# A two-layer diffusion backbone on one core: unread products at the start, two weights loaded earlier, a short softplus chain moved

## The chip, the core and the metric

The program runs on one core of a Trainium2 chip. The core has five engines that each take their own queue of instructions in order: TensorE (PE in the profile, its weight loads PEld), VectorE (DVE), ScalarE (ACT), GpSimd (POOL) and SyncE (SP). SP issues nearly all transfers between memory and the core here. An engine waits for another one, or for a transfer, at a semaphore. The metric is the device time of one execution in microseconds; less is better. TensorE's array has two clock levels in these traces, 1.2 and 2.4 GHz.

## What is computed

The reference runs two layers over 256 context tokens and 512 latent tokens of width 1024. Cut to what matters for the start of the first layer:

```python
shift, scale, gate = _adaln(c, ada_w[layer], ada_b[layer])      # silu(c) @ w + b, three parts
shift_c, scale_c, gate_c = _adaln(c_ctx, ada_w[layer], ada_b[layer])
h_l = _rmsnorm(x, norm_g[layer]) * (1.0 + scale[:, None]) + shift[:, None]
h_c = _rmsnorm(cx, norm_g[layer]) * (1.0 + scale_c) + shift_c
z = jnp.concatenate([h_c, h_l], axis=1) @ w_in                  # first step of the even mixer
...
log_a = -LRU_C * r.astype(jnp.float32) * jax.nn.softplus(-lam.astype(jnp.float32))
```

Everything after that (latent attention, the recurrent scan, the second layer's neighbourhood attention, the output projections and the final norm) is the same before and after the change.

## The kernel before

Tokens lie along the free axis and channels on the 128 partitions, so the input is eight tiles `x0` to `x7` of 128x768, with columns 0 to 511 for the latent (LAT) and 512 to 767 for the context (CTX). A product that wants nearly float32 accuracy is made of three passes in a fast format: weights and activations are split into a high part (`h`, a rounded copy, on ScalarE) and a low part (`l`, the rest, on VectorE), and `z_t` (L141) adds high x high, high x low and low x high into one PSUM tile. Such a pass is a pair of products, one with 512 columns and one with 256. For each 128 outputs there are 8 blocks k of channels, so 24 pairs.

The start of the program, which is all that the change touches, goes as follows.

1. SP loads `x0` to `x7`, then weights. A modulation chunk is two transfers of 512 KB (`ada.._0r` and `ada.._4r`).
2. ScalarE squares the x tiles and VectorE adds them up (`acc`, L365). TensorE sums over channels (`pssum`, L296), a root and its reciprocal follow, and TensorE spreads them over the partitions (`r00b`, L322). That gives `rsb`.
3. TensorE multiplies the conditioning vectors by the modulation weights (`psada`, L215, 32 outputs wide, float32). ScalarE copies the result (`rows`, L227), TensorE turns it (`psc`, L232), VectorE makes shift and factor of it (`av`, `as`, `am`, L234 to L250). `ada_prep1`/`ada_go1` do so for one block of channels; `ada_prep`/`ada_go` for a whole chunk pair, which gives two blocks: chunks 1 and 5 give blocks 2 and 3, chunks 2 and 6 give 4 and 5, chunks 3 and 7 give 6 and 7.
4. `hb(j, c)` makes block j of the modulated input: VectorE scales x (L338), ScalarE adds the shift and rounds (`hh`, L340), VectorE makes the rest (`hl`, L341).
5. TensorE multiplies each block, as it comes, by three weights: `w0t0` (into `psx0`), `w0t1` (`psx1`) and `w0t8` (`psg8`). These 72 pairs are here called the first three projections. After them VectorE copies `psx0` out (`lx0`, L537, L539), and only then may `psx2`, which uses the same PSUM banks, begin.
6. `softplus` of the recurrence's decay is a chain of 18 operations of VectorE on 128x8 values (`sp`, L504 to L515). Its result is first read by the gates of the recurrence, after the first projections.

The code names the order in which work is asked for, and a scheduler in the framework moves instructions within each engine's queue; `behind(engine)` and `issue_after(instruction)` keep it from moving work ahead of a given instruction. What the queue of each engine holds in the end is fixed when the program is built.

Of the kernel before, what the change touches and what calls it, by code (L numbers as in the profile page):

```python
# [11 lines left out]
F32 = mybir.dt.float32  # L12
# [4 lines left out]
ALU = mybir.AluOpType  # L17
# [29 lines left out]
def build(nc, tc, A, out, dbg=None):  # L47
# [4 lines left out]
    V, S, P, G, SY = nc.vector, nc.scalar, nc.tensor, nc.gpsimd, nc.sync  # L52
    PE, ACT, DVE = mybir.EngineType.PE, mybir.EngineType.Activation, mybir.EngineType.DVE

    def f(ap):
        return ap.bitcast(F32)

    def dump(name, ap):
        if dbg is not None and name in dbg:
            SY.dma_start(dbg[name], ap)  # L60
# [3 lines left out]
    def pool(name, bufs, **kw):  # L64
        cm = tc.tile_pool(name=name, bufs=bufs, reuse_waits="tile", **kw)
        p = cm.__enter__()
        pools.append((name, cm))
        return p
# [28 lines left out]
    def small(tag, name, n=1, dt=F32):  # L97
        return sm.tile([128, n], dt, tag=tag, name=name, bufs=SM.get(tag))

    HE = (G,)  # L100
    HTN = 2
    FE = V
# [3 lines left out]
    vec = cst.tile([128, NV], F32, name="vec")  # L106
    SY.dma_start(vec, A["vecs"])
    junk = cst.tile([128, 768], BF16, name="junk")

    def col(i, n=1):  # L110
        return vec[:, i : i + n]

    def load_w(name, src, shape, new=None):
        raw = (new or t4)(name + "r", shape, F32, "r")
        SY.dma_start(raw, src)
        return raw

    def split_raw(name, raw, shape, new=None, eng=V, heng=S):
        hi = (new or t4)(name + "h", shape, F32R, "h")
        if heng is S:  # L120
            S.activation(hi, raw, AF.Copy)
        else:
            heng.tensor_copy(hi, raw)
        lo = (new or t4)(name + "l", shape, F32R, "l")
        eng.tensor_tensor(lo, raw, f(hi), ALU.subtract)
        return hi, lo

    def split_w(name, src, shape, new=None, eng=V, heng=S):
        return split_raw(name, load_w(name, src, shape, new), shape, new, eng, heng)

    def kfun(hl, n=None):
        h, l = hl
        return (lambda k: h[:, k], lambda k: l[:, k])
# [19 lines left out]
    pzz2 = pool("pzz2", 1, space=PSUM)  # L153
    pa = pool("pa", 2, space=PSUM)
    pzz3 = pool("pzz3", 1, space=PSUM)
    zpools, zcount = [pzz, pzz2], [0]

    def zz(name):
# [9 lines left out]
    def ada_load(l, ch, new=None, step=4):  # L168
        return [
            load_w(f"ada{l}_{ch}_{k}", A["ada"][l, ch, :, k : min(k + step, 8)], (min(step, 8 - k), 256), new)  # L170
            for k in range(0, 8, step)
        ]
# [25 lines left out]
    def behind(*engines):  # L198

        stack = ExitStack()  # L200
        for e in engines:
            stack.enter_context(tc.issue_after(next(i for i in reversed(nc.cur_bb.bb.instructions) if i.engine == e)))
        return stack
# [38 lines left out]
    def ada_cols(l, j, raws, pp, pin=False, n=2):  # L242

        step = ada_rows(l, j, raws, pp, pin, n)
        yield next(step)
        v = next(step)
        V.tensor_tensor(ashf[l][:, j : j + n], v[:, :, 0:2], bc2(vec, V_ADAB + 24 * l + j, n), ALU.add)
        d = amul[l][:, j : j + n]
        V.tensor_tensor(d, v[:, :, 2:4], bc2(badd, 24 * l + 8 + j, n), ALU.add)
        V.tensor_tensor(d, d, bc2(vec, V_NG + 8 * l + j, n), ALU.mult)  # L250
# [84 lines left out]
    def h_block(l, j, c, x, rsb, hh, hl, pieces):  # L335

        a, s = amul[l][:, j, c : c + 1], ashf[l][:, j, c : c + 1]
        V.scalar_tensor_tensor(x, x, a, rsb, ALU.mult, ALU.mult)  # L338
        for i, o in pieces:
            S.activation(o(hh), i(x), AF.Identity, bias=s)  # L340
            V.scalar_tensor_tensor(o(hl), i(x), s, f(o(hh)), ALU.add, ALU.subtract)  # L341
# [35 lines left out]
    wt = {}  # L377

    def prep_t(ft):
        wt[ft] = kfun(split_w(f"w0t{ft}", A["w0t"][ft], (8, 128)))  # L380

    def x_t(ft):
        ps = zz(f"psx{ft}")
        z_t(both(ps), wt.pop(ft), hh, hl, 8)
        return ps
# [3 lines left out]
    def ada_prep(ch):  # L389
        ada_w[ch] = ada_load(0, ch, t4a)  # L390
# [5 lines left out]
    def ada_prep1(j):  # L396
        ada_w["half", j] = [[load_w(f"ada0{j}{m}", A["ada0"][j, m], (8, 128), t4a)] for m in range(2)]

    def ada_go1(j):
        for _ in ada_cols(0, j, ada_w.pop(("half", j)), paa, n=1):  # L400
            pass

    def hb(j, c):
        w = (LAT, CTX)[c]
        pc_ = [(lambda ap: ap, lambda ap: ap[:, w])]
        h_block(0, j, c, x_tiles[j][:, w], rsb0[:, w], hh[j], hl[j], pc_)
# [13 lines left out]
    norm0c = norm0()  # L420
    hh = [th(f"hh{j}", F32R) for j in range(8)]
    hl = [th(f"hl{j}", F32R) for j in range(8)]
    raw0 = load_w("w0t0", A["w0t"][0], (8, 128))
    ada_prep1(1)
    ada_go1(0)
    hb(0, 0)
    norm0c()
    with behind(PE, ACT):
        wt[0] = kfun(split_raw("w0t0", raw0, (8, 128)))
        hb(0, 1)  # L430
        ada_prep(1)
        ada_go1(1)
    hb(1, 0)
    hb(1, 1)
    ada_prep(5)
    ada_prep(2)
    ada_go(1)
# [11 lines left out]
    hb(5, 0)  # L449
    hb(5, 1)  # L450
    hb(6, 0)
    prep_t(1)
    hb(6, 1)
    hb(7, 0)
    hb(7, 1)
    prep_t(8)
    psx.append(x_t(0))
    psx.append(x_t(1))
    psg8 = zz3("psg8")
# [37 lines left out]
    sp4 = cst.tile([128, 8], F32, name="sp4")  # L497
    nsp4 = cst.tile([128, 8], F32, name="nsp4")

    nl, e, z, w, q = (small("sp", f"sp{i}", 8) for i in range(5))  # L500
    V.tensor_scalar(nl, col(V_LAM, 8), -1.0, None, ALU.mult)
    V.tensor_tensor(e, nl, col(V_LAM, 8), ALU.min)
    S.activation(e, e, AF.Exp)
    V.tensor_scalar(z, e, 2.0, None, ALU.add)  # L504
    V.reciprocal(z, z)
    V.tensor_tensor(z, z, e, ALU.mult)
    V.tensor_tensor(w, z, z, ALU.mult)
    V.tensor_scalar(q, w, 1.0 / 19, None, ALU.mult)
    for d in range(17, 1, -2):
        V.scalar_tensor_tensor(q, q, 1.0 / d, w, ALU.add, ALU.mult)  # L510
    V.scalar_tensor_tensor(q, q, 1.0, z, ALU.add, ALU.mult)
    V.tensor_scalar(nl, nl, 0.0, None, ALU.max)
    V.scalar_tensor_tensor(sp4, q, 2.0, nl, ALU.mult, ALU.add)
    V.tensor_scalar(nsp4, sp4, -4.0, None, ALU.mult)
    V.tensor_scalar(sp4, sp4, 4.0, None, ALU.mult)  # L515
    dump("sp4", sp4)

    SEG = ((0, NC), (NC, NT))
# [1323 lines left out]
```

## Time and profile before

| | us |
|---|---|
| median of 3 runs | 779.3 (778.96 to 779.54) |
| the profiled execution's own time | 780.51 |
| its span, first to last instruction | 778.7 |
| TensorE busy in the span | 742.4 (95%) |
| VectorE, ScalarE, GpSimd busy | 507.5, 415.6, 163.7 |

The profiled execution took 1.8 us more than its span, which lies before the first and behind the last instruction. Times inside the trace count from the start of the span. A row of the timeline stands for several equal instructions in sequence; its length runs from the start of the first to the end of the last, and on TensorE the last one's end lies behind the start of the next row, since products are pipelined. The price of a row there is the distance from its start to the next row's start.

### The profile page before, as it was taken

The numbers are of one execution on the slowest core, as the hardware profiler recorded it, in microseconds if no ns is written. First come the engines' busy times: TensorE is split into PE (matmuls) and PEld (weight loads), VectorE is DVE, ScalarE is ACT, GpSimd is POOL, SyncE is SP. The second block draws the span as 40 slices with busy tenths as digits, with TensorE's granted clock in tenths as the row PEclk, the third lists the DMA queues.
The fourth block names the chain that finished last, engine by engine and source line by source line (L and its number), as shares of the span: only waits on it lengthen the run. The fifth ranks groups of instructions, "written<-read, shape, count | busy, mean of one in ns | idle before, by whom it ended". The sixth has DMA issues, their size and how long they took to land.

```text
span 778.7 us, 13220 instructions
## 1 busy us (share of the span) xinstructions
PE 742.4 (95%) x4966; PEld 652.8 (84%) x4966; DVE 507.5 (65%) x1051; ACT 415.6 (53%) x811; POOL 163.7 (21%) x191
## 2 busy tenths in 40 slices
PE   2999999999999999999999999999999999999995
PEld 2678898787788877888998899888888799889995
DVE  5748499887478777753396567546653766568544
ACT  5424867964467777542245355535542645456633
POOL 0000002003153477404210022002200211021414
PEclk9999999999999999999999999999999999999998
DMA  8913403411455553257021550236124541336203
GB/s 332 407 49 109 134 28 122 162 42 28 118 157 141 177 169 126 89 172 261 28 82 46 144 163 16 91 113 190 38 99 140 174 120 55 109 102 170 82 1 109
DMA packets 33598, 95.29 MB, mean 122 GB/s; under 512 B 4608, under 2 KB 6784, under 8 KB 33536
## 3 DMA queue, kind: packets, MB, share of 16 engines
q1 hardware_dynamic: 32960, 93.93, 37.5%
q8 instruction: 39, 0.64, 0.3%
q10 hardware_dynamic: 576, 0.52, 0.2%
q14 instruction: 23, 0.19, 0.1%
HBM read 73.99 MB, written 4.19 MB: 100 GB/s over the span
## 4 chain that ended last, share of the span: by engine, by line
PE 75%; DVE 12%; ACT 5%; issue 4%; DMA 3%; POOL 1%; SPq 0%; POOLq 0%; ACTq 0%; DVEq 0%
PE psg L141 11%; PE psv L1270 8%; PE psq L141 7%; PE w0oy L1175 7%; PE pskl L141 6%; PE psx L141 4%; PE w1oy L1175 4%; PE pt L1387 3%; PE pskc L141 3%; PE psada L215 2%; PE s L1346 2%; PE s L808 2%; PE s L1347 2%; PE po L1370 2%; PE po L1371 2%
## 5 line engine op out<-in xcount | busy, mean ns | idle before, releaser
L764 POOL TENSOR_SCALAR p<-p,rc 128x512 f32<-128x512 f32 (+1 forms) x96 | 77.7, 812 | 325.8 <-DVE rc L763 309.7
L1354 ACT ACTIVATE p<-s,nm 128x512 f32<-128x512 f32 x64 | 43.8, 686 | 37.0 <-DVE nm L1352 20.6
L1390 DVE TENSOR_TENSOR ptl<-pt,pth 128x512 fp32r<-128x512 f32 x64 | 43.6, 687 | 26.7 <-ACT pth L1389 26.7
L1389 ACT ACTIVATE pth<-pt 128x512 fp32r<-128x512 f32 x64 | 37.3, 595 | 34.7 <-PE pt L1387 25.5
L1352 DVE CUSTOM_DVE_ANT_1 s<-s,bias 128x512 f32<-128x512 f32 x48 | 33.2, 696 | 16.3 <-PE s L1347 14.3
L1387 PE MATMUL pt<-ident,p 128*128 128x128 f32 x256 | 40.0, 272 | 0.0
L615 POOL TENSOR_TENSOR mix<-mix,la 128x256 f32<-128x256 f32 x4 | 3.6, 905 | 172.8 <-DVE la L609 124.8
L844 DVE TENSOR_TENSOR pt<-pt,pt 128x512 fp32r<-128x512 f32 x48 | 31.9, 681 | 11.5 <-ACT pt L843 11.4
L843 ACT ACTIVATE pt<-pt 128x512 fp32r<-128x512 f32 x48 | 27.4, 595 | 16.1 <-PE pt L881 16.0
L763 DVE RECIPROCAL rc<-rs 128x1 f32<-128x1 f32 x96 | 15.2, 158 | 31.6 <-ACT p L1354 22.2
L1346 PE MATMUL s<-k,q 128*128 128x256 f32 x128 | 34.3, 292 | 0.4 <-DMA q<-qx 0.2
L812 ACT ACTIVATE p<-s,nm 128x768 f32<-128x768 f32 x32 | 28.8, 901 | 10.7 <-DVE nm L810 10.4
L1387 PEld LDWEIGHTS pt<-ident,p 128*128 128x128 f32 x256 | 31.1, 140 | 4.0 <-issue 0.4
L810 DVE TENSOR_REDUCE nm<-s 128x1 f32<-128x768 f32 x32 | 30.4, 951 | 4.6 <-PE s L808 4.1
L1347 PE MATMUL s<-k,q 128*128 128x256 f32 x128 | 33.3, 284 | 0.0
L1370 PE MATMUL po<-pth,v 128*128 128x256 f32 (+1 forms) x96 | 31.6, 335 | 0.0
L1371 PE MATMUL po<-ptl,v 128*128 128x256 f32 (+1 forms) x96 | 29.6, 324 | 0.0
L881 PE MATMUL pt<-ident,p 128*128 128x128 f32 x192 | 28.7, 273 | 0.0
L862 PE MATMUL po<-pt,v 128*128 128x256 f32 x96 | 26.1, 296 | 1.7 <-DVE pt L844 1.6
L861 PE MATMUL po<-pt,v 128*128 128x256 f32 x96 | 26.6, 294 | 0.4 <-DVE rcc L763 0.4
L1346 PEld LDWEIGHTS s<-k,q 128*128 128x128 f32 x128 | 24.3, 190 | 3.0 <-issue 1.4
L1200 ACT ACTIVATE sq<-xr 128x512 f32<-128x512 f32 (+1 forms) x16 | 8.2, 522 | 33.1 <-DVE xr L1181 27.1
(966 smaller groups left out, 2636.8 us busy)
## 6 DMA issues: line engine op xcount, KB each, us to landing
ada_0r<-ada SPq DMA_DIRECT2D x22, 512.0 KB, 5.0
ada_4r<-ada SPq DMA_DIRECT2D x22, 512.0 KB, 5.4
q<-qx SPq DMA_DIRECT2D x32, 256.0 KB, 5.0
bias<-bias SPq DMA_DIRECT2D x16, 256.0 KB, 2.7
x<-xin SPq DMA_DIRECT2D x8, 384.0 KB, 6.3
xr<-xin SPq DMA_DIRECT2D x8, 384.0 KB, 7.0
x1d<-xr SPq DMA_DIRECT2D x8, 256.0 KB, 5.2
x<-x1d SPq DMA_DIRECT2D x8, 256.0 KB, 4.2
```

The costliest lines, as they stand in the source:

```text
L141: P.matmul(ps, a(k), b[k][:, c], start=(k == 0 and i == 0), stop=(k == nk - 1 and i == 2),)
L764: G.tensor_scalar(p, p, rc, 0.5, ALU.mult, ALU.mult)
L1175: P.matmul(ps, a, b[k][:, c], start=(n == m == 0 and ps is dst[0][0] and not second), stop=(n == 7 and m == 2), skip_group_check=True,)
L1270: P.matmul(ps, tok(a[k], t), b[:, k % 4], start=(k == 0 and i == 0), stop=(k == 7 and i == 2))
L1346: P.matmul(s[:, :256], lhs, kap, start=(i == 0), stop=False, skip_group_check=True)
L1347: P.matmul(s[:, 256:], lhs, k2[:, CTX], start=False, stop=(i == 1), skip_group_check=True)
L1354: S.activation(p, s, AF.Exp, bias=nm, scale=-1.0, accum_out=rsum)
L1370: P.matmul(dst, vv, h, start=first, stop=False, skip_group_check=True)
L1371: P.matmul(dst, vv, l, start=False, stop=last, skip_group_check=True)
L1387: P.transpose(ps[:, 128 * j : 128 * j + 128], p1[hd, b][:, 128 * c : 128 * c + 128], ident)
L1389: S.activation(h, ps, AF.Copy)
L1390: V.tensor_tensor(l, ps, f(h), ALU.subtract)
```

## The change

Three edits.

- 51 products of 128x512 in bf16, of a tile `junk` that GpSimd fills with ones, stand first in TensorE's queue. They write a PSUM tile that nothing reads.
- `w0t1` and `w0t8` are loaded (`load0t`) right behind the single-block modulation weights, ahead of the whole chunks, and their split (`split0t`) stands behind block 1 of h. Before, the code asked for them behind block 6, and the scheduler moved them up to where the queues below show them.
- All but the first two VectorE operations of softplus stand behind the last `hl` of block 7 (`h_mark`). Before, the scheduler had put them at the front, between the sums of squares.

```diff
+    WARM = 51
...
     junk = cst.tile([128, 768], BF16, name="junk")
+    G.memset(junk[:, :512], 1.0)
...
+    idle = pa.tile([128, 512], F32, tag="a", name="idle")
+    for _ in range(WARM):
+        P.matmul(idle, junk[:, :128], junk[:, :512], start=True, stop=True)
...
-    raw0 = load_w("w0t0", A["w0t"][0], (8, 128))
+    raw = {}
+
+    def load0t(ft):
+        raw[ft] = load_w(f"w0t{ft}", A["w0t"][ft], (8, 128))
+
+    def split0t(ft):
+        wt[ft] = kfun(split_raw(f"w0t{ft}", raw[ft], (8, 128)))
+
+    load0t(0)
     ada_prep1(1)
+    load0t(1)
+    load0t(8)
     ada_go1(0)
     hb(0, 0)
     norm0c()
     with behind(PE, ACT):
-        wt[0] = kfun(split_raw("w0t0", raw0, (8, 128)))
+        split0t(0)
         hb(0, 1)
         ada_prep(1)
         ada_go1(1)
     hb(1, 0)
     hb(1, 1)
+    with behind(DVE):
+        split0t(8)
+    split0t(1)
     ada_prep(5)
...
     hb(6, 0)
-    prep_t(1)
     hb(6, 1)
     hb(7, 0)
     hb(7, 1)
-    prep_t(8)
+    h_mark = next(i for i in reversed(nc.cur_bb.bb.instructions) if i.engine == DVE)
...
-    V.tensor_scalar(z, e, 2.0, None, ALU.add)
...
+    with tc.issue_after(h_mark):
+        V.tensor_scalar(z, e, 2.0, None, ALU.add)
...
```

The scheduler answers to these edits with another order of TensorE's queue as well. The place that matters most is where the second-last step of the modulation, `psc0_6` (it turns the result of chunks 3 and 7, from which blocks 6 and 7 of h are made), stands among the products. In the kernel before it stands inside the products of block 4:

```order
L141 MATMUL psg8_539<-hh4_189,w0t8h_437 128x512
L141 MATMUL psx0_441<-hh4_189,w0t0h_249 128x256
L141 MATMUL psx1_490<-hh4_189,w0t1h_422 128x256
L141 MATMUL psg8_539<-hh4_189,w0t8h_437 128x256
L232 MATMUL psc0_6_403<-ident_67,rows0_6_401 128x128 x2
L141 MATMUL psx0_441<-hl4_197,w0t0h_249 128x512
L141 MATMUL psx1_490<-hl4_197,w0t1h_422 128x512
```

In the changed kernel (line numbers there are a few higher):

```order
L221 MATMUL psada0_6_449<-ada0_7_4r_414,c34_162 32x256 x4
L143 MATMUL psx1_543<-hh5_243,w0t1l_355 128x512
L143 MATMUL psx1_543<-hh5_243,w0t1l_355 128x256
L143 MATMUL psg8_592<-hl5_251,w0t8h_349 128x256
L143 MATMUL psg8_592<-hh5_243,w0t8l_351 128x512
L143 MATMUL psg8_592<-hh5_243,w0t8l_351 128x256
L238 MATMUL psc0_6_468<-ident_67,rows0_6_466 128x128 x2
L143 MATMUL psx0_494<-hh6_244,w0t0h_306 128x512
L143 MATMUL psx1_543<-hh6_244,w0t1h_353 128x512
```

So `psc0_6` now stands behind all products of blocks 0 to 5, directly ahead of the first product that reads block 6. The four halves of chunks 3 and 7 (`psada0_6`), which stood in a row before, now stand one by one among the products of blocks 3 to 5. Those of chunks 1 and 5 stand one by one as well, where three of them stood in a row, and three of chunks 2 and 6, which stood one by one, now stand in a row behind `psc0_2`.

On VectorE, at the end of the modulated input, the kernel before goes straight from block 7 to the copy of `psx0`:

```order
L341 SCALAR_TENSOR_TENSOR hl7_200<-x7_102,as0_116,hh7_192 128x256
L537 COPY lx0_645<-psx0_441 128x256
L539 COPY lx0_645<-psx0_441 128x8x48
L539 COPY lx0_645<-psx0_441 128x8x2x8
L125 TENSOR_TENSOR w0t2l_672<-w0t2r_668,w0t2h_670 128x1024
```

The changed kernel has the chain of softplus between them:

```order
L347 SCALAR_TENSOR_TENSOR hl7_253<-x7_155,as0_169,hh7_245 128x256
L523 TENSOR_SCALAR sp2_673<-sp1_672 128x8
L531 TENSOR_SCALAR sp0_671<-sp0_671 128x8
...
L529 SCALAR_TENSOR_TENSOR sp4_675<-sp4_675,sp3_674 128x8 x8
L530 SCALAR_TENSOR_TENSOR sp4_675<-sp4_675,sp2_673 128x8
L532 SCALAR_TENSOR_TENSOR sp4_669<-sp4_675,sp0_671 128x8
L533 TENSOR_SCALAR nsp4_670<-sp4_669 128x8
L534 TENSOR_SCALAR sp4_669<-sp4_669 128x8
L556 COPY lx0_698<-psx0_494 128x256
```

That is 18 operations, each but one waiting for the one ahead of it. On SP's queue the two weights take the places of the first chunk in the changed kernel:

```order
L117 DMA ada011r_258<-ada0 128x1024
L117 DMA w0t1r_260<-w0t 128x1024
L117 DMA w0t8r_262<-w0t 128x1024
L117 DMA ada0_1_0r_313<-ada 128x1024
L117 DMA ada0_1_4r_315<-ada 128x1024
L117 DMA ada0_5_0r_357<-ada 128x1024
L117 DMA ada0_5_4r_359<-ada 128x1024
L918 DMA ropen_697<-ropen 128x256
```

Before, `w0t1r` and `w0t8r` stood between `ada0_5_4r` and `ropen`, so that the four halves of chunks 1 and 5 each move two places back. Behind these rows the two queues agree, but for the halves of chunk 7, which stand one and two places later.

## Rows read from the trace of the kernel before

**Rows 1.** The page: busy time of TensorE, its weight loads beside it.

```profile
PE 742.4 (95%) x4966; PEld 652.8 (84%) x4966; DVE 507.5 (65%) x1051; ACT 415.6 (53%) x811; POOL 163.7 (21%) x191
```

**Rows 2.** Timeline of TensorE, 14 to 28 us: start, length, what, idle before.

```profile
14.46 1.08 PE L215 MATMUL psada<-ada000r,c 128*32 128x128 f32 x16 [14.46 <-DVE acc L365]
...
23.23 1.01 PE L141 MATMUL psx<-hh,w0t0h 128*128 128x512 f32 x2 [0.48 <-ACT hh L340]
...
27.03 0.61 PE L141 MATMUL psx<-hl,w0t0h 128*128 128x512 f32 x2
```

**Rows 3.** Timeline of SP: issue of two transfers.

```profile
5.50 0.43 SPq L115 DMA_DIRECT2D ada000r<-ada  x1
...
12.09 0.33 SPq L115 DMA_DIRECT2D ada_4r<-ada  x1
```

**Rows 4.** DMA issues of 5 to 6 and 12 to 13 us: last number, us to landing.

```profile
ada000r<-ada SPq DMA_DIRECT2D x1, 512.0 KB, 8.8
...
ada_4r<-ada SPq DMA_DIRECT2D x1, 512.0 KB, 9.9
```

**Rows 5.** Windows: PE, PEld, DVE, ACT, POOL busy, PEclk, DMA share, GB/s.

```profile
40.00:45.00 5.00, 5.00 (x43) 3.76 (x46) 0.48 (x4) 0.38 (x1) 0.00 (x0) 1.00 0.26 103
...
771.00:774.50 3.50, 0.66 (x2) 0.29 (x2) 2.13 (x9) 0.38 (x1) 1.58 (x3) 0.50 0.18 62
```

**Rows 6.** Timeline of ScalarE: the rounding of one weight.

```profile
29.92 1.05 ACT L121 ACTIVATE w0t8h<-w0t8r 128x1024 fp32r<-128x1024 f32 x1
```

**Rows 7.** Timeline of TensorE: one modulation half alone between product pairs.

```profile
32.89 0.52 PE L141 MATMUL psx<-hh,w0t1l 128*128 128x512 f32 x2
33.34 0.64 PE L215 MATMUL psada<-ada_0r,c 128*32 128x256 f32 x8
33.91 0.61 PE L141 MATMUL psg<-hh,w0t8l 128*128 128x512 f32 x2
34.36 0.51 PE L141 MATMUL psg<-hh,w0t8h 128*128 128x512 f32 x2
```

**Rows 8.** Timeline of all engines: from `psc` to the first product of block 4.

```profile
44.03 0.38 PE L232 MATMUL psc<-ident,rows 128*128 128x128 f32 x2
...
44.45 0.19 DVE L234 TENSOR_REDUCE av<-psc 128x8 f32<-128x32 f32 x1 [6.79 <-PE psc L232]
...
44.80 0.61 PE L215 MATMUL psada<-ada_4r,c 128*32 128x256 f32 x8
...
45.14 2.21 DVE L338 SCALAR_TENSOR_TENSOR x<-x,am,rsb 128x512 f32<-128x512 f32 x4
...
45.23 0.62 PE L215 MATMUL psada<-ada_0r,c 128*32 128x256 f32 x8
...
45.93 1.12 ACT L340 ACTIVATE hh<-x,as 128x512 fp32r<-128x512 f32 x2 [4.84 <-DVE x L338]
...
46.70 0.50 PE L141 MATMUL psx<-hh,w0t0h 128*128 128x512 f32 x1 [0.43 <-ACT hh L340]
```

**Rows 9.** Timeline of TensorE: first products of blocks 2 and 6, and of `psx2`.

```profile
36.07 0.50 PE L141 MATMUL psx<-hh,w0t0h 128*128 128x512 f32 x1
...
53.41 0.40 PE L141 MATMUL psx<-hh,w0t0h 128*128 128x512 f32 x1
...
59.96 0.58 PE L141 MATMUL psx<-hh,w0t2h 128*128 128x512 f32 x2
```

**Rows 10.** Timeline of VectorE: the end of h, and seven operations of softplus.

```profile
4.49 1.37 DVE L510 SCALAR_TENSOR_TENSOR sp<-sp,sp 128x8 f32<-128x8 f32 x7
...
49.94 2.21 DVE L338 SCALAR_TENSOR_TENSOR x<-x,am,rsb 128x512 f32<-128x512 f32 x4
52.06 2.20 DVE L341 SCALAR_TENSOR_TENSOR hl<-x,as,hh 128x512 fp32r<-128x512 f32 x4
58.73 0.42 DVE L537 COPY lx<-psx 128x256 f32<-128x256 f32 x1 [4.46 <-PE psx L141]
```

**Rows 11.** Timeline of GpSimd: the fill of a tile.

```profile
0.91 0.33 POOL L188 MEMSET c<- 128x272 f32 x1
```

More of the change, by code (lines that the diff above doesn't have):

```diff
@@ L503, in build @@
     S.activation(e, e, AF.Exp)
-    V.tensor_scalar(z, e, 2.0, None, ALU.add)
[L505 to L515, printed above, removed]
+    with tc.issue_after(h_mark):
+        V.tensor_scalar(z, e, 2.0, None, ALU.add)
+        V.reciprocal(z, z)
+        V.tensor_tensor(z, z, e, ALU.mult)
+        V.tensor_tensor(w, z, z, ALU.mult)
+        V.tensor_scalar(q, w, 1.0 / 19, None, ALU.mult)
+        for d in range(17, 1, -2):
+            V.scalar_tensor_tensor(q, q, 1.0 / d, w, ALU.add, ALU.mult)
+        V.scalar_tensor_tensor(q, q, 1.0, z, ALU.add, ALU.mult)
+        V.tensor_scalar(nl, nl, 0.0, None, ALU.max)
+        V.scalar_tensor_tensor(sp4, q, 2.0, nl, ALU.mult, ALU.add)
+        V.tensor_scalar(nsp4, sp4, -4.0, None, ALU.mult)
+        V.tensor_scalar(sp4, sp4, 4.0, None, ALU.mult)
     dump("sp4", sp4)
```

## The prediction, made before the changed kernel ran

> **What bounds the kernel now.** I read the page first: TensorE is busy for 742.4 of 778.7 us [rows 1], so what moves TensorE's queue moves the end, unless a later wait swallows it. The edits all lie before 60 us. I therefore read TensorE's timeline there, then the loads it waits for, then the steps of VectorE and ScalarE between its products.
>
> The reader is to see four things. First, TensorE does nothing until 14.46 [rows 2]. The wait is put down to VectorE's sums, but the operand `ada000r`, issued at 5.50, lands 8.8 later, at 14.3 [rows 3, 4]: a transfer sets the start, and no edit moves it. Second, TensorE runs slowly at first. Two products of the same shapes take 1.01 at 23.23 and 0.61 at 27.03 [rows 2]; a row's length has the pipeline's fill in it, so this is the step from 1.2 to 2.4 GHz, although the profile's clock column reads 1.00 from the start. So the array needed 12.6 us from its first product, of which 3.8 us from the first wide one, to come to full speed. Third, from 36.07 to 59.96 TensorE works through blocks 2 to 7 at full speed with one visible wait, 0.43 ahead of block 4 [rows 8, 9]. Fourth, `psx2` begins at 59.96, 1.23 behind the copy `lx0`, which began at 58.73 when `psx0` was done [rows 9, 10]. All loads of this stretch are in by about 41.3 (a share of 0.26 in 40 to 45 [rows 5]), before TensorE needs them.
>
> **Prices.** A pair of products at full speed: 18 pairs in 59.96 - 53.41 = 6.55, so 0.36 [rows 9]. A modulation half alone between pairs: 33.91 - 33.34 = 0.57, and the pair ahead of it and the one behind it each take 0.45, 0.09 over a plain one: 0.75 in all [rows 7]. The same half in a row of its like: 45.23 - 44.80 = 0.43 [rows 8]. From a `psc` to the first product of its block, when nothing fills the gap: 46.70 - 44.03 = 2.67, of which x begins after 45.14 - 44.03 = 1.11 [rows 8]. From the start of a pair of x blocks to the end of the last `hl`: 52.06 + 2.20 - 49.94 = 4.32 [rows 10]. One operation of softplus in the chain: 1.37 / 7 = 0.2 [rows 10].
>
> **The unread products.** GpSimd filled 128x272 in 0.33 from 0.91 [rows 11]; the fill of `junk` stands near there, so I let them start at 1.4. The trace has no bf16 product. At full speed two thirds of a pair's 0.36 is 0.24 for 512 columns, at the lower level twice that. All at full speed they end at 1.4 + 51 x 0.24 = 13.6; all at the lower level at 25.9. I take the 3.8 us of wide products that preceded full speed as the slow part, 8 products, and 43 fast ones: 1.4 + 3.8 + 10.3 = 15.5, 1.0 behind the first real operand. The Trainium skill ("TensorE: Matmul & The Clock Gate", Back-to-back issue gap) gives 0.427 and 0.216 for 512 columns at the two levels; by it the same 51, 8 of them slow, end at 14.1 and delay nothing. No run here shows a bf16 product yet, so the value from rows stands in the sum.
>
> Does a delay of 1.0 cost? Behind it lies the stretch from the first product to the first of block 0, 23.23 - 14.46 = 8.77 [rows 2], made of TensorE's steps and of small steps of ScalarE and VectorE between them. If none of it shrinks at the higher clock, block 0 begins at 24.2; if all of it halves, at 19.9. With half of it TensorE's, it shrinks by a quarter to 6.6, and block 0 begins at 15.5 + 6.6 = 22.1. Three pairs with `w0t0`: 23.2. There the next product needs the rounded `w0t8`. That weight takes the queue place of the transfer issued at 12.09 and landed at 22.0 [rows 3, 4], and its rounding takes 1.05 [rows 6]: 23.1. So delay and load end together, and I go on from 23.2. The ends are 23.1 (the load alone) and 25.3 (nothing shrinks).
>
> **The early weights and the new order of TensorE.** From 23.2, TensorE has 15 of the 18 pairs of blocks 0 and 1 (5.4) and the four halves of chunks 1 and 5, each alone (3.0): `psc0_2` at 31.6. The wait behind it, 2.67, takes three halves of chunks 2 and 6 under it. Block 2 begins at 34.3, 1.8 before its 36.07. This lead is what the clock and the earlier weights are worth here; no load is nearer than that, since the four halves move two places back, to places of transfers that TensorE had long used by then.
>
> From block 2 to `psx2` it was 23.9 before [rows 9]. Of that falls away: one half that is already done, 0.75, and the wait of 0.43. To it come: the four halves of chunks 3 and 7 alone instead of in a row, 4 x (0.75 - 0.43) = 1.3, and the wait behind `psc0_6`. Before, `psc0_6` had the rest of two blocks of products to cover what follows it. Now the next product is the first of block 6 itself, so all 2.67 is bare but for the 0.3 of `psc` (counted before too): 2.4. Sum: 23.9 - 0.75 - 0.43 + 1.3 + 2.4 = 26.4, and TensorE alone would come to `psx2` at 60.7. The lead is spent.
>
> **Softplus behind h.** At its old place it cost nearly nothing: its operations lay in the gaps between sums that wait for squares, ahead of a start which a transfer sets. At the new place: block 6 begins 6.55 before 60.7, at 54.15; `psc0_6` 2.67 earlier, at 51.5; x begins at 52.6, `hl7` ends at 56.9, 18 x 0.2 = 3.5 of softplus end at 60.4. `psx0` is ready at 60.7 - 1.23 = 59.5. So `lx0` waits for 0.9, and with it, on VectorE's queue, the low part of `w0t2`; TensorE waits for both. `psx2` begins at 60.4 + 1.23 = 61.6, against 59.96: **1.6 later**. The cover here was 4.46, VectorE's wait before `lx0` [rows 10]; it would hide the chain, but it was that long because h ran ahead of TensorE, which it no longer does behind a bare `psc0_6`.
>
> Behind 61.6 the work is the same and TensorE nearly full, so I carry the 1.6 to the end; the ends are none of it and all of it. Profiled execution: 780.51 + 1.6 = 782.1. That execution lies 1.2 above the median shown, so the timed value is 779.3 + 1.6 = **780.9**.
>
> **Rivals.** A difference of 0.2%, 1.56 us, is about what a measurement of this kernel tells from none.
>
> *Lone halves cost what they cost in a row* (not slower). Nine halves stand alone now; if the 0.32 over 0.43 comes from their old neighbours and not from standing alone, 9 x 0.32 = 2.9 falls away, and the time is 779.3 + 1.6 - 2.9 = 778.0. It decides for no slowdown from 0.18 a half on. Against it: the pairs on both sides take longer by the same 0.09 [rows 7].
>
> *The chain is hidden after all* (the moved softplus costs nothing). If TensorE comes out of block 6 and 7 later than 6.55 by the 0.9, say since `hl6` is not ready when the products of `hh6` are through, VectorE is done in time and only TensorE's 60.7 counts: 780.0, no difference.
>
> *The clock falls again* (slower). Between the last unread product and block 0 there are some 7 us of narrow products, sums and transposes. The trace does show a fall: at the end of the program, where TensorE mostly waits for the last norm, the clock stands at 0.50 in 771.0 to 774.5 [rows 5]. If it falls before block 0, the 3.8 us of block 0 run slowly as before, 1.9 lost, and the stretch ahead shrinks less, some 0.8 more: 783.6. The Trainium skill (same page, Why this matters for your kernels) says that idle gaps between bursts take the array back to the lower level; the row at the end agrees, and no row here shows it between bursts.
>
> *The unread products stay slow* (slower). If they need the 12.6 us that the start needed, 26 of them run slowly and 25 fast: 1.4 + 12.6 + 6.0 = 20.0, 4.5 behind my 15.5, and all of it on the path: 785.4.
>
> **How the numbers follow.** Forecast 0.42; lone halves cheap 0.30, rather more than half of it beyond 777.7, since VectorE's chain then starts earlier too; chain hidden 0.12; clock falls 0.11; products slow 0.05. The forecast's own range is 780.0 to 782.0. Faster by over 0.2%: the larger part of the lone halves, 0.18. Slower by over 0.2%: rather more than half of the forecast and the last two, 0.39. Within: the rest, 0.43. The range leaves out the slow products, half of the falling clock and the lower third of the lone halves: 777.5 to 783.5.
>
> **What would show it.** Right: first product of block 2 near 34.3, of block 6 near 54 with an idle TensorE of over 2 us ahead of it, put down to `hh`; 18 softplus rows between `hl` and `lx`, with `lx0` near 60.4 and no wait for TensorE; `psx2` near 61.6. Wrong: block 6 begins before 52 (halves cheap, or the lead larger), or `lx0` waits for `psx0` (chain hidden), or the first pairs of block 0 take 1.0 again (clock), or `psada` begins behind 16 (products slow). The forecast falls as a whole if TensorE's 1.6 is gone again by 130 us.

## The result, and the profile after

The changed kernel takes 785.33 us (median of 4 runs, 784.89 to 786.46), beside 779.13 of the kernel before on the same chip: ratio 1.0083 [1.0065, 1.0100]. It is 6.2 us slower, and outside the range of the prediction. The profiled execution took 786.46, its span is 784.7 against 778.7, so the two profiles show the same difference.

TensorE's timeline after. Columns as in the rows before: start, length, engine, line and operands, and in brackets the idle time ahead with what ended it.

```profile
1.46 13.10 PE L161 MATMUL idle<-junk 128*128 128x512 bf16 x51 [1.46 <-POOL eps L186]
14.48 0.64 PE L221 MATMUL psada<-ada000r,c 128*32 128x128 f32 x16
...
20.75 0.51 PE L143 MATMUL psx<-hh,w0t0h 128*128 128x512 f32 x1 [0.83 <-ACT hh L346]
...
23.97 1.01 PE L143 MATMUL psg<-hh,w0t8h 128*128 128x512 f32 x2 [0.22 <-ACT w0t8h L123]
...
34.73 0.38 PE L238 MATMUL psc<-ident,rows 128*128 128x128 f32 x2
...
37.41 0.50 PE L143 MATMUL psx<-hh,w0t0h 128*128 128x512 f32 x1 [0.86 <-ACT hh L346]
37.75 0.40 PE L143 MATMUL psx<-hh,w0t1h 128*128 128x512 f32 x1
37.99 0.40 PE L143 MATMUL psg<-hh,w0t8h 128*128 128x512 f32 x1
...
54.18 0.38 PE L238 MATMUL psc<-ident,rows 128*128 128x128 f32 x2
56.85 0.80 PE L143 MATMUL psx<-hh,w0t0h 128*128 128x512 f32 x1 [2.29 <-ACT hh L346]
57.45 0.63 PE L143 MATMUL psx<-hh,w0t1h 128*128 128x512 f32 x1
57.88 0.63 PE L143 MATMUL psg<-hh,w0t8h 128*128 128x512 f32 x1
...
65.16 0.59 PE L143 MATMUL psx<-hh,w0t2h 128*128 128x512 f32 x2 [0.32 <-DVE lx L558]
```

Against [rows 2, 9]: the array starts early and is done with the unread products at 14.48, so they delay nothing. Block 0 begins 2.5 earlier than before (20.75 against 23.23). But block 2 begins 1.3 later (37.41 against 36.07) and `psx2` 5.2 later (65.16 against 59.96). The pair at 23.97 takes 1.01, as a slow one did before, and the second product of block 6 takes 0.43 from its start to the next one's (57.45 to 57.88) where the same product of block 2 takes 0.24 (37.75 to 37.99). So the clock is to be read next.

The windows of the same execution: stretch, its length, busy time of each engine, and then the granted clock (1.00 is 2.4 GHz, 0.50 is 1.2 GHz), share of the DMA engines, GB/s.

```profile
19.03:22.44 3.41, 2.01 (x24) 1.06 (x20) 3.31 (x6) 2.23 (x5) 0.00 (x0) 1.00 1.04 410
22.44:29.27 6.83, 6.61 (x29) 3.54 (x28) 5.08 (x11) 3.02 (x4) 0.00 (x0) 0.50 1.03 404
29.27:53.15 23.88, 23.02 (x176) 15.79 (x172) 10.85 (x25) 5.92 (x11) 0.00 (x0) 1.00 0.54 211
53.15:56.57 3.42, 1.41 (x11) 0.98 (x7) 1.87 (x7) 0.88 (x2) 0.00 (x0) 1.00 0.00 0
56.57:59.99 3.42, 3.14 (x9) 2.65 (x10) 3.38 (x10) 1.69 (x4) 0.00 (x0) 0.50 0.00 0
```

The clock falls twice before the end of the program. Ahead of each fall TensorE (the first number behind the length) has little to do: it is busy for 2.01 of 3.41 us at the end of the narrow modulation and in the first products of block 0, and for 1.41 of 3.42 around the bare wait behind `psc0_6`. Then it is slow for 6.83 and 3.42 us of nearly full work. Half of that, 3.4 and 1.7, is the most that the two falls can cost; what of it lies on TensorE's path is worked out below.

VectorE at the end of the modulated input, which answers to [rows 10]:

```profile
57.41 2.20 DVE L347 SCALAR_TENSOR_TENSOR hl<-x,as,hh 128x512 fp32r<-128x512 f32 x4
59.53 0.17 DVE L523 TENSOR_SCALAR sp<-sp 128x8 f32<-128x8 f32 x1
...
62.79 0.17 DVE L534 TENSOR_SCALAR sp<-sp 128x8 f32<-128x8 f32 x1
63.92 0.42 DVE L556 COPY lx<-psx 128x256 f32<-128x256 f32 x1 [0.97 <-PE psx L143]
```

The 18 operations of softplus stand where they were expected and take 3.4 us, from 59.53 to 62.96, but `lx0` still waits 0.97 for TensorE behind them: they are hidden.

### The profile page after: what moved, and what is told of

It is laid out like the page before. It is cut to its first block, busy times and chain, and to the rows that moved or that the text cites. A ratio compares the mean times of both kernels' runs of the same rounds, so it can differ in the third digit from the quotient of the medians.

```text
span 784.7 us, 13317 instructions
## 1 busy us (share of the span) xinstructions
PE 756.0 (96%) x5017; PEld 657.2 (84%) x5017; DVE 508.0 (65%) x1051; ACT 416.1 (53%) x811; POOL 164.3 (21%) x192
## 4 chain that ended last, share of the span: by engine, by line
PE 73%; DVE 11%; ACT 5%; DMA 4%; issue 4%; POOL 1%; SPq 1%; POOLq 0%; ACTq 0%; DVEq 0%
PE psg L143 11%; PE psv L1289 8%; PE w0oy L1194 7%; PE psq L143 6%; PE pskl L143 6%; PE psx L143 5%; PE w1oy L1194 4%; PE pt L1406 3%; PE pskc L143 3%; PE s L827 2%; PE s L1365 2%; PE psada L221 2%; PE s L1366 2%; PE po L1390 2%; PE po L1389 2%
## 5 line engine op out<-in xcount | busy, mean ns | idle before, releaser
L782 DVE RECIPROCAL rc<-rs 128x1 f32<-128x1 f32 x96 | 15.3, 159 | 31.4 <-ACT p L1373 22.1
```

## The experiments

Ratios are to the kernel before on the same chip, with 95% intervals.

**One edit at a time.** The first four kernels take the change apart.

`e1_products`: the kernel before with the first edit alone.

```diff
+    G.memset(junk[:, :512], 1.0)
...
+    for _ in range(WARM):
+        P.matmul(idle, junk[:, :128], junk[:, :512], start=True, stop=True)
```

> The kernel before with the 51 unread products alone; the loads and softplus stand where they stood, and the scheduler keeps psc0_6 inside the products of block 4. Clock theory (the loss of the changed kernel is two falls of TensorE's clock, at 22.4 and 56.6): the narrow stretch ahead of block 0 is the same, so the clock falls once near there and nearly all of the products' gain is lost again, but nothing waits long behind psc0_6 and there is no second fall: 777 to 779. Order theory (the loss is the new order, with a bare wait and lone halves; the clock costs little): without the new order the gain of the products remains, 775 to 776. If the products themselves are the loss: 782 or more.

781.64, ratio 1.0017 [1.0008, 1.0027]. The products alone cost 1.3 us (the kernel before takes 780.30 on this chip). That lies outside all three forecasts, nearest to the last. The one fall that the clock theory foresaw is there, ahead of block 0:

```profile
14.50:18.15 3.65, 3.06 (x46) 2.53 (x35) 1.85 (x12) 0.87 (x4) 0.00 (x0) 1.00 1.02 409
18.15:21.57 3.42, 3.19 (x41) 1.78 (x42) 3.20 (x8) 2.98 (x6) 0.00 (x0) 0.50 1.03 407
21.57:60.00 38.43, 36.70 (x254) 26.07 (x255) 24.43 (x55) 14.92 (x24) 0.00 (x0) 1.00 0.56 218
```

`psc0_6` keeps its cover in this kernel (33 pairs stand behind it, as before), and `psx2` begins at 58.15, 1.8 ahead of [rows 9]; at the end of that execution, one of the two shortest of ten, only 0.2 of the lead is left. Of the rest, 1.08 is a wait of a product `s` near 632 for the load of `q`, which the kernel before does not have there: the four loads are issued 1.2 earlier (623.41 against 624.57), but the slowest takes 6.2 us to land, and not 5.1.

`e3_softplus`: the kernel before with the third edit alone.

```diff
+    h_mark = next(i for i in reversed(nc.cur_bb.bb.instructions) if i.engine == DVE)
...
+    with tc.issue_after(h_mark):
+        V.tensor_scalar(z, e, 2.0, None, ALU.add)
```

> The kernel before with softplus behind the last block of h alone. VectorE waits 4.46 ahead of lx0 there and the chain takes 3.5: both theories say no change, 779.1 within 0.5. If the chain stands in the way of lx0, 780 or more.

780.25, ratio 1.0001 [0.9992, 1.0011]: the move of softplus costs nothing by itself. `lx0` waits 1.30 for `psx0` behind it. The start of this kernel differs from the one before only in where softplus stands, yet in its profile `psx2` begins at 58.68 and not at 59.96. The difference stands at `psc0_2` already (27.81 against 29.13). So ahead of `psc0_2` single profiles differ by as much as 1.3 us.

`e4_no_products`: the changed kernel without the first edit.

> The changed kernel without the 51 products: early loads and softplus behind h. The scheduler then puts psc0_6 behind half of block 5's products, 21 pairs ahead of psx2, so its wait is covered. Clock theory: one rise, no fall before the end, about the time before: 778.5 to 780.5. Order theory, in which early loads and lone halves cost: 782 to 784.

782.78, ratio 1.0034 [1.0021, 1.0048]. In TensorE's queue 21 pairs stand behind `psc0_6`, three of them ahead of block 6, and not 18 with none ahead; the wait is there, but smaller:

```profile
52.70 0.50 PE L141 MATMUL psx<-hh,w0t0h 128*128 128x512 f32 x1 [0.89 <-ACT hh L340]
```

and the clock stays at 1.00 from 22.8 to 60. The time is the one that the order theory gave (782 to 784), and not the clock theory's: with no slow stretch ahead of 60, the earlier loads and the order that comes with them cost 2.5 us. Where they do stays open: in this profile `psx2` begins at 59.90, no later than before, and the clock falls at 309.5 for 3.4 us. The products and the loads together (1.0083) cost more than the two apart (1.0017 and 1.0034): with both, the scheduler leaves `psc0_6` bare.

`e5_no_softplus`: the changed kernel with softplus at its old place.

> The changed kernel with softplus at its old place; TensorE, ScalarE and SP have the same order as in the changed kernel. Both theories: lx0 waits for TensorE in the changed kernel, not for softplus, so nothing moves: 785.3 within 0.7. If softplus is part of the loss: 784.4 or less.

787.02, ratio 1.0096 [1.0075, 1.0116], which overlaps the changed kernel's. The clock falls in the same two places, 3.4 us long at 22.6 and at 56.8, and once more at 312.8. Moving softplus back wins nothing, so no part of the loss is seen to be softplus's.

**Filling the stretches in which the clock falls.** The next kernels add unread bf16 products of 256 columns, so the array works on while nothing else changes. `fill` writes a part of a PSUM tile that nothing reads.

```diff
+    def fill(ps, key):
+        for _ in range(FILL.get(key, 0)):
+            P.matmul(ps[:, 256:512], junk[:, :128], junk[:, :256], start=True, stop=True)
...
             pm = ada_mm(raws, pp, f"psada{l}_{j}", wd)
+            fill(pm, ("mm", l, j))
...
                 P.transpose(ps[:, 128 * i : 128 * i + 128], rows[:, 128 * i : 128 * i + 128], ident)
+            fill(ps, ("sc", l, j))
```

`e6_fill_wait`: 18 behind `psc0_6`, `FILL = {("sc", 0, 6): 18}`.

> The changed kernel with 18 unread products of 256 columns behind psc0_6, inside the wait for block 6; they end before hh6 is ready, so the wait itself stays. Clock theory: the second fall (56.6 to 60.0) goes away and block 6 runs at full speed: 1.7 less than the changed kernel, ratio to the kernel before about 1.006. Order theory (a bare wait costs its length, the clock little): no change, ratio 1.008.

789.61, ratio 1.0110 [1.0077, 1.0142]: no better. It didn't fill the wait but lengthened it. The products stood in the tile of `psc0_6`, and VectorE's sum `av` waited for them; the bare wait came behind:

```profile
51.60 0.38 PE L244 MATMUL psc<-ident,rows 128*128 128x128 f32 x2
51.82 2.13 PE L230 MATMUL psc<-junk 128*128 128x256 bf16 x18
56.24 0.80 PE L144 MATMUL psx<-hh,w0t0h 128*128 128x512 f32 x1 [2.29 <-ACT hh L353]
```

So it doesn't test whether a filled wait keeps the clock up. Its profile shows the fall behind a bare wait once more, at 56.1 for 3.4 us, and that TensorE waits for this path.

`e7_fill_narrow`: 4, 6 and 4 in the narrow stretch, `FILL = {("mm", 0, 0): 4, ("mm", 0, 1): 6, ("sc", 0, 1): 4}`.

> The changed kernel with 4, 6 and 4 unread products of 256 columns in the narrow stretch between the 51 products and block 0, in places where TensorE waits. Clock theory: if they hold the clock up, the first fall (22.4 to 29.3) goes away: 3.4 less than the changed kernel, ratio to before about 1.004; if they are too few, no change. Order theory: no change, ratio 1.008 or a little more.

785.18, ratio 1.0054 [1.0030, 1.0078]. The first slow stretch in the profile is 3.40 long, from 18.1 to 21.5, and the second one stays. That the first is shorter than the changed kernel's 6.83 is not shown to be the fill's work: `e5_no_softplus` and `e6_fill_wait`, with the changed kernel's queue of TensorE there and no fill, have 3.4 as well. What the fill is worth is read below from five pairs of kernels.

`e8_fill_both`: both of them.

> Both fills in the changed kernel. Clock theory: what is left is the new order alone, as the prediction's sum had it: ratio to before 1.001 to 1.003. Order theory: 1.008.

786.66, ratio 1.0087 [1.0061, 1.0112], with the fault of `e6_fill_wait`. Both falls are in its profile, at 18.0 and 58.9.

`e9_prod_fill`: `e1_products` with the fill of the narrow stretch.

> The kernel before with the 51 products and the fills of the narrow stretch, no early loads, softplus at its old place; psc0_6 stays covered. Clock theory: TensorE runs at full speed from block 0 on, 3 us more are gained at lx0 than with the products alone, ratio to before 0.996 to 0.998. If the loss lies behind 60 us whatever the start does (as with the products alone, which were 1.8 ahead at lx0 and 1.3 behind at the end of the typical run): 1.000 to 1.002.

780.47, ratio 0.9994 [0.9978, 1.0010]. No slow stretch up to 306, but none of the 3 us more either: `psx2` begins at 58.35, 1.6 ahead of the kernel before and 0.2 behind `e1_products`, with waits of TensorE of 0.49 and 0.44 for the two parts of `w0t1` on the way. It isn't a gain that could be measured. In its profile the clock also falls in the middle of the program, behind a wait of 2.14 for `p`,

```profile
303.00:306.50 3.50, 1.36 (x11) 1.08 (x10) 1.14 (x3) 2.49 (x5) 2.74 (x2) 1.00 0.03 9
306.50:309.90 3.40, 3.40 (x16) 3.21 (x16) 3.01 (x7) 2.92 (x6) 2.69 (x4) 0.50 0.32 99
```

and half of the 3.40, 1.7, is as much as the lead was.

`e10_fill_free`: the fill behind `psc0_6` put right. It writes the tile of `psada0_6`, which is read by then.

```diff
-            fill(ps, ("sc", l, j))
+            fill(pm, ("free", l, j))
```

> The changed kernel with 18 unread products of 256 columns behind psc0_6, this time into the tile of psada0_6, which nothing reads any more, so that VectorE does not wait for them as it did in e6_fill_wait; they take about 2.1 us of the 2.3 to 2.7 that TensorE stands still. Clock theory (the clock falls because of the bare wait): the second slow stretch is gone, block 6 keeps 0.36 a pair, lx0 and psx2 come 1.7 earlier than in the changed kernel (near 62.2 and 63.4), and the ratio falls from 1.0083 to about 1.006. Rival (the slow stretch is set off by something else, as the narrow products ahead of the wait, or comes anyway): the stretch stays, ratio 1.008.

784.76, ratio 1.0056 [1.0034, 1.0078]. VectorE no longer waits, block 6 begins 2.67 behind `psc0_6` as in the changed kernel, and runs at full speed:

```profile
54.34:57.01 2.67, 2.35 (x22) 1.87 (x20) 2.15 (x7) 0.77 (x2) 0.00 (x0) 1.00 0.00 0
57.01:64.00 6.99, 6.83 (x36) 5.55 (x36) 5.94 (x24) 2.78 (x5) 0.00 (x0) 1.00 0.00 0
```

The second slow stretch is gone. `psx2` begins at 64.21, 0.95 earlier than in the changed kernel and not 1.7. In time the gain isn't clear: the interval overlaps the changed kernel's. Three of the six runs took 782.5 to 782.8 at a mean granted clock of 0.994 or 0.995, three 786.7 to 786.9 at 0.989 or 0.990. The profiled one took 786.72 and shows the first slow stretch at its full length, 22.3 to 29.1, and a fall at 312.5.

**Covering the wait with work of the kernel.** `e12_cover`: nine pairs of `psg8`, those of blocks 3 to 5, stand behind `psc0_6`; the work is the same.

```diff
     ada_go(3)
+    c_mark = next(i for i in reversed(nc.cur_bb.bb.instructions) if i.engine == PE)
...
         for k in range(nk):
+            with tc.issue_after(mark) if mark is not None and k >= 3 else ExitStack():
```

> The changed kernel with the nine pairs of psg8 for blocks 3 to 5 held behind psc0_6, so that 27 pairs and not 18 stand behind it and none of the work is added or left out. Nine pairs are 3.2 us, more than the 2.67 from psc to the first product of its block. Theory (the bare wait costs its own 2.3 and, by the clock, 1.7 more): no idle TensorE over 0.5 behind psc0_6, no second slow stretch, psx2 about 4 earlier than in the changed kernel (near 61), ratio about 1.003. Rival 1 (the wait is the modulation's own lateness and only moves): a wait of about 2 stands elsewhere ahead of psx2, ratio 1.008. Rival 2 (the softplus chain comes to the front, since h and TensorE are then closer): lx0 waits for VectorE, psx2 about 1 to 2 earlier, ratio 1.006.

783.18, ratio 1.0039 [1.0025, 1.0053]. The wait behind `psc0_6` is gone, and with it the second fall (the third row is VectorE's copy `lx0`, the others are TensorE's):

```profile
48.78 0.44 PE L239 MATMUL psc<-ident,rows 128*128 128x128 f32 x2 [0.57 <-ACT rows L234]
48.98 0.59 PE L144 MATMUL psg<-hh,w0t8h 128*128 128x512 f32 x2
...
52.19 0.39 PE L144 MATMUL psx<-hh,w0t0h 128*128 128x512 f32 x1
...
57.74 0.42 DVE L558 COPY lx<-psx 128x256 f32<-128x256 f32 x1 [0.94 <-PE psx L144]
...
58.97 0.59 PE L144 MATMUL psx<-hh,w0t2h 128*128 128x512 f32 x2 [0.34 <-DVE sp L532]
```

Block 6 finds its operand ready. `psx2` begins at 58.97, 6.2 earlier than in the changed kernel; 2.4 of that stands at `psc0_2` already (32.27 against 34.73), since in this execution, the shortest of six, the clock did not fall ahead of block 0 either, although TensorE's queue there is the changed kernel's. The bracket of `psx2` names softplus (`sp`), but that is no sign of the second rival: `lx0` waits 0.94 for TensorE and not for VectorE, the operation named stands behind the copies in VectorE's queue, and the wait is as long as the changed kernel's 0.32 for the copy.

`e13_cover_narrow`: the same with the fill of `e7_fill_narrow`.

> The same as e12_cover, and with it the 4, 6 and 4 unread products of 256 columns in the narrow stretch ahead of blocks 0 and 1 (as in e7_fill_narrow), so that both places where the clock fell are filled or covered. Theory: no slow stretch between 22 and 65, psx2 2 to 3.5 earlier than in e12_cover, near 58, ahead of the 59.96 of the kernel before; ratio 0.999 to 1.001 if the lead is kept as little as in e9_prod_fill, 0.997 if it is kept whole. Rival (the two slow stretches are not what is left of the loss, but the loads and the order are): ratio at or above 1.003.

781.94, ratio 1.0016 [1.0007, 1.0025]. No slow stretch before the end of the program, and `psx2` at 59.16, not the 58 that was expected but 0.2 behind `e12_cover`. The ratio lies between the forecast and the rival. With both places filled or covered, 0.0067 of the loss of 0.0083 is gone.

`e11_free_narrow`: the fills of `e7_fill_narrow` and `e10_fill_free` together.

> The changed kernel with unread products in both places where the clock fell: the 4, 6 and 4 of e7_fill_narrow in the narrow stretch, and the 18 of e10_fill_free behind psc0_6. TensorE still has nothing of its own to do behind psc0_6, so against e13_cover_narrow, where real products stand there, only the bare wait is left: 2.1 to 2.6 us, ratio 1.0016 + 0.003 = 1.0046 at most, no slow stretch between 22 and 65 in the profile. Rival (18 narrow bf16 products don't hold the clock in every run: e10_fill_free had three runs near 782.6 and three near 786.8): again two groups some 4 us apart, and a slow stretch behind the wait in a profile of the slower group.

783.48, ratio 1.0041 [1.0025, 1.0057]. In its profile one slow stretch of 3.4 is left ahead of block 0 and none behind `psc0_6`. Against `e13_cover_narrow` it is 0.0025 slower, 2.0 us, about the bare wait without the clock; the intervals just touch. All six runs lie between 782.9 and 785.2, so the groups of `e10_fill_free` don't come back.

**The profiles side by side.** These kernels have the same work from `psc0_2` to `psx2`, but for what fills or covers the wait for block 6 and, in `e5_no_softplus`, the place of softplus. `psc0_2` is the step of the modulation ahead of block 2:

| kernel | low clock ahead of `psc0_2` | `psc0_2` | `psx2` | between |
|---|---|---|---|---|
| changed | 22.4 to 29.3 | 34.73 | 65.16 | 30.43 |
| `e5_no_softplus` | 22.6 to 26.0 | 33.20 | 64.07 | 30.87 |
| `e7_fill_narrow` | 18.1 to 21.5 | 32.48 | 63.19 | 30.71 |
| `e10_fill_free` | 22.3 to 29.1 | 34.91 | 64.21 | 29.30 |
| `e11_free_narrow` | 18.0 to 21.4 | 33.07 | 62.34 | 29.27 |
| `e12_cover` | none | 32.27 | 58.97 | 26.70 |
| `e13_cover_narrow` | none | 32.45 | 59.16 | 26.71 |

In the last column, the first three have the bare wait and the second fall, the next two the wait without the fall, the last two neither. So the wait costs 2.6 and the fall behind it 1.1 to 1.6. In the third column, a slow stretch of full length costs up to 2.5.

**What the narrow fill is worth.** Five pairs of kernels differ in its 14 products and in what the scheduler moves with them: one transpose and one product near block 0 in four pairs, some more products of blocks 0 and 1 in the pair of `e9_prod_fill`. The kernel with the fill is faster each time: by 0.0029 (`e7_fill_narrow` against the changed kernel), 0.0023 (`e9_prod_fill` against `e1_products`), 0.0023 (`e8_fill_both` against `e6_fill_wait`), 0.0023 (`e13_cover_narrow` against `e12_cover`) and 0.0015 (`e11_free_narrow` against `e10_fill_free`). Within a pair the intervals touch or overlap; that all five point one way is the evidence. None of the five profiles with the fill has a slow stretch behind 22 ahead of `psc0_2`.

## Why the prediction was wrong

The order of the work was read rightly, and most prices held. **The step that failed is that all work behind 15.5 was priced at full speed.** The rival that doubted it, that the clock falls again, had 0.11, one place and 2.7 us (783.6 instead of 780.9). The traces show two places, which put TensorE 2.4 and 1.8 us behind the forecast; of the 4.2, some 3.5 go with the clock. The measured 785.3 is nearly the 785.4 of the rival in which the unread products stay slow, and that is chance: 10 of them began slowly, not 26, and `psada` began at 14.48, not behind 16.

- *The unread products.* Forecast: they end at 15.5. Measured: 14.48, so the price of 0.24 a product was too high. Block 0 at 22.1: measured 20.75. The Trainium skill ("TensorE: Matmul & The Clock Gate", Back-to-back issue gap) gave 14.1 here as an estimate, and the trace agrees with its prices: 0.427 from start to start at the lower level and 0.216 at the higher one.
- *The load of `w0t8`.* Forecast: rounded at 23.1, and that the load and not the products sets the first pair of `psg8`. Measured: issued at 11.90, landed 10.9 later, rounded at 23.9, and TensorE's pair at 23.97. Right, late by 0.8. Had the clock held, TensorE would only have waited longer here.
- *From there to `psc0_2`.* Forecast 8.4 us, measured 34.73 - 23.97 = 10.8. The clock stood at 0.50 until 29.27; half of 29.27 - 23.97 is 2.65, which is the difference and a little more. `e12_cover`, with the same queue up to `psc0_2` and no fall, comes there 2.5 earlier. This is the first half of the failure: the array's early start was undone by the fall behind it. The five pairs show it from the other side, by 0.0015 to 0.0029. But the queue alone doesn't set this fall: with the same one, the profiles have 6.8 us of it (changed kernel, `e10_fill_free`), 3.4 (`e5_no_softplus`, `e6_fill_wait`) or none (`e12_cover`), and what decides between them is not shown.
- *The bare wait behind `psc0_6`.* Forecast 2.67 from `psc` to the first product, with over 2 us idle put down to `hh`. Measured 56.85 - 54.18 = 2.67, with 2.29 idle. Right to the digit. Without the clock, the wait is worth 2.0 in the times of `e11_free_narrow` and `e13_cover_narrow` and 2.6 in their profiles; the forecast had 2.4.
- *What follows the wait.* Forecast 6.55 for the 18 pairs of blocks 6 and 7. Measured 65.16 - 56.85 = 8.31, which is 1.8 more. Of that, 1.1 goes when the clock holds: `e10_fill_free` and `e11_free_narrow` take 7.20. The other 0.65 stands without the clock too; it is of the kind that the rival of the hidden chain named (blocks 6 and 7 take longer than 6.55), and no run takes it apart. That the second fall hangs on the wait is shown twice, by covering the wait (`e12_cover`, `e13_cover_narrow`) and by unread products in it that leave TensorE's order as it is (`e10_fill_free`, `e11_free_narrow`): in all four profiles the clock stays at 1.00 there, and in the five with a bare wait (the changed kernel and `e5` to `e8`) it falls. That a wait has this second price was not in the forecast at all.
- *Softplus.* Forecast: VectorE comes 0.9 after TensorE. Measured: TensorE comes 0.97 after VectorE, since blocks 6 and 7 take longer. This is the rival that the chain is hidden, mostly with the slow clock in the place of the late `hl6` that it named. `e3_softplus` and `e5_no_softplus` show no price. Where the wait is covered (`e12_cover`), `lx0` still waits 0.94 for TensorE.
- *Lone halves.* No gain in them: 0.57 a row, as in [rows 7].

The sum at `psx2`: 65.16 - 61.6 = 3.6 over the forecast. The load is 0.8 of it, the stretch ahead of `psc0_2` 2.4 and the one behind the wait 1.8; against these, softplus's 0.9 falls away, and 0.4 between blocks 2 and 6. From `psx2` to the end the loss grows from 5.2 to 6.0. Part of that stands near 255: the loss is 5.30 at a product `s` (253.33, before 248.03) and 6.21 at the transposes `pt` behind it (256.17, before 249.96), by two waits for the split of the transposed scores, which the order before has in hand by then:

```profile
254.98 0.39 PE L880 MATMUL po<-pt,v 128*128 128x256 f32 x1 [0.36 <-ACT pt L862]
255.71 0.38 PE L881 MATMUL po<-pt,v 128*128 128x256 f32 x1 [0.34 <-DVE pt L863]
```

**What stays open.** `e13_cover_narrow`, with no slow stretch in its profile and no bare wait, is still 0.0016 above the kernel before, 1.2 us, though the spans of the two profiled executions are equal (778.7). No single row carries that: its profiled execution is the shortest of eleven, so what the others lose stands in no trace. `e4_no_products` (1.0034) says that the earlier loads and their order cost something without the clock; a kernel with them alone, softplus left in its place, was not run. And the wait for `p` between 305 and 314, of 1.7 to 2.4, stands in the profile of every kernel here, the one before too; in eight of the fourteen the clock falls behind it, in the kernel before and the changed one it doesn't. What decides that, the runs did not settle. At 1.7 a fall it is as large as the lead that the array's early start could bring. No version came out measurably ahead of the kernel before.

## What to carry to other kernels

A wait of TensorE is to be priced twice: by its length, and by what the work behind it costs if the clock falls there; here the wait cost 2.6 and the fall 1.1 to 1.6. Work put in front to raise the clock is only worth what the stretch between it and the first heavy products keeps; here the products alone ended 1.3 us behind the kernel without them. And when edits change the scheduler's order, look for the instruction that a later block hangs on: nine pairs of the kernel's own work behind `psc0_6` took away half of the loss.

## What the hardware showed that was not expected

The clock fell without a long idle time: the longest wait ahead of the first fall was 0.83, in a stretch in which TensorE was busy for 2.01 of 3.41 us, and ahead of the second 2.29. The Trainium skill (same page, Why this matters for your kernels) speaks of idle gaps between bursts; these rows agree that the level falls between bursts. They also show it behind narrow work with short waits, though not in every execution: in `e12_cover` the clock held through the same stretch.

The profile's clock column reads 1.00 also where the array has not yet come to full speed for the first time: in the first 3.9 us of the changed kernel 10 unread products begin, 0.43 apart, under a 1.00.

```profile
1.46:5.40 3.94, 3.94 (x10) 1.46 (x11) 1.04 (x7) 1.47 (x4) 0.57 (x3) 1.00 0.74 235
5.40:14.48 9.08, 9.08 (x43) 3.94 (x41) 5.84 (x7) 7.51 (x10) 0.00 (x0) 1.00 1.01 374
```

In the second row the others follow at 0.22. The start of [rows 2] was slow under the same column. So there the length of a product has to be read, not the column.
